# The heads' input projection in pairs of tiles, the last 512 tokens by one level of Strassen's scheme, with four token groups and four shared PSUM banks

## The chip, the cores and the metric

The kernel runs on one core of one Trainium2 chip. The metric is the device time of one execution in microseconds (us), the median over runs. PE is TensorE's matmul side (PEld its weight loads), DVE is VectorE, ACT is ScalarE, POOL is GpSimd, SP is SyncE. A "raw" number is float32. The kernel holds each float32 operand of the projection as two float32r tiles, `hi` (the value rounded) and `lo` (the rest), and a product is three matmuls: hi·hi, hi·lo and lo·hi.

## What is computed

One decoder layer over 1040 tokens (16 meta tokens and 1024) of width 1024. The input projection `proj = a @ w_in` gives 28 tiles of 128 columns: dq, dk, dv (differential attention, four heads each) and hq, hf, hi, hg (HGRN, four heads each). Everything behind it stays as it was.

```python
a = rmsnorm(h, ln_mix_pre[l])
proj = a @ w_in[l]
dq, dk, dv, hq, hf, hi, hg = jnp.split(proj, SPLITS, axis=-1)
y_diff = diff_attention(dq, dk, dv, diff_lambda[l], diff_subln[l], rel_bias_table, lam_init)
y_hgrn = hgrn2(hq, hf, hi, hg, lb_all[l], hgrn_gnorm[l])
mix = jnp.concatenate([y_diff, y_hgrn], axis=-1) @ w_out[l]
h = h + rmsnorm(mix, ln_mix_post[l])
a = rmsnorm(h, ln_ffn_pre[l])
y = conv_ffn(a, w_ffn_up[l], ffn_conv_w[l], ffn_conv_b[l], w_ffn_down[l])
h = h + rmsnorm(y, ln_ffn_post[l])
```

## The kernel before, in words

The tokens stand in nine blocks (16 meta tokens, then eight of 128). For the projection they form three groups of columns, `GROUPS`: blocks 0 to 2 (272 columns), 3 to 5 and 6 to 8 (384 each). The normed input lies transposed in `ahi` and `alo`, eight slabs `k` of 128 rows. A projected tile is a 128-column stripe of `w_in`: for each group 8 slabs × 3 matmuls into one PSUM bank (`proj_group`, line 236, and `proj_step`, line 244), then the tile's own evacuation (`ev_q`, `ev_k`, `ev_v`, `ev_f`, `ev_i`, `ev_g`), which copies the bank to SBUF on ScalarE and VectorE. Values are turned to token rows by transposes afterwards (`to_nat`, line 376; PSUM tile `pn_va` or `pn_vh`), through a list `late` that `flush` empties.

The work has these stages.

The prologue (up to 51.23 us) loads x and the weights, norms the input group by group, and makes dq, dk, dv of head 0 at the same time. Its order is written out by hand and kept on all engines (`state["ordered"]`). For each group: `x_stats` squares the rows on ScalarE and takes the root there (`rstd_of`), the diagonals `dg` are made on ScalarE and VectorE, `x_spread` turns them with a matmul into `prs`, `x_norm` multiplies on VectorE, `x_hi` casts on ScalarE, `x_lo` subtracts on GpSimd. `Kinds` holds the three tiles' matmuls.

The heads (51.23 to 489 us) alternate: four phases of attention with the tiles hf, hq, hi, hg of the same head as dense work, and three phases of HGRN with dq, dk, dv of the next head. `interleave` (line 65) takes a step of the side work, then as many dense matmuls as the fill `FA` = 840 or `FH` = 800 allows, each charged max(115, 0.42 × columns). `dense` (line 791) loads and splits the next tile's weights (`load_split`: cast on ScalarE, subtraction on GpSimd) one tile ahead. PE's order is the order in which the program issues (`manual_schedule`); the other engines get a scheduler's order, and each runs its list in that order. In the heads PSUM holds two banks for the projected tiles (`ip`), two for the small matmuls of the sides (`m`), and two double banks for scores (`S`; block 8's last 512 keys are `E`).

An attention step for block i is: scores S on PE, near-diagonal bias added on VectorE, maximum on VectorE, exponential on ScalarE to `pb`, scaling of pb on VectorE, transposes `pt` on PE, copies `at`, products `pa` on PE. An HGRN step multiplies `kr` and `hq` on VectorE and feeds small matmuls `pl`.

The out-projection, FFN up and FFN down follow; the change does not touch them. SyncE and GpSimd issue the sums of down weights (`tsc`) during the heads.

Of the kernel before, what the change touches and what calls it, by code (L numbers as in the profile page):

```python
# [17 lines left out]
P = 128  # L18
# [12 lines left out]
GROUPS = [(0, 3), (3, 6), (6, 9)]  # L31
# [4 lines left out]
WARM = 26  # L36

# [7 lines left out]


def place(t):
    return t + (0 if t < start(3) else 16)
# [43 lines left out]
def layer_kernel(ctx: ExitStack, tc: tile.TileContext, x, meta, xt, relative, lbl, gpre, gpost, win,  # L92
# [23 lines left out]
    deep = {"ip": 3, "m": 5}  # L116
# [28 lines left out]
    def ps_in(name):  # L145
        return pp.tile([P, 512], F32, tag="ip", name=name, bufs=deep["ip"])

    def ps_m(name):
        return pp.tile([P, 512], F32, tag="m", name=name, bufs=deep["m"])
# [47 lines left out]
    gap(atp, "edge", 64)  # L197
    ahi, alo = (atp.tile([P, KD, P * NBLK], F32R, tag=t, name=t) for t in ("ahi", "alo"))
# [34 lines left out]
    def load_m(m, name, where=None, bufs=4):  # L233
        return [load_split(win[m][:, 512 * c: 512 * (c + 1)], f"{name}_{c}", where, bufs) for c in range(2)]

    def proj_group(g, parts, name, evac):
        b0, b1 = GROUPS[g]
        t0, t1 = start(b0), start(b1 - 1) + P
        n = t1 - t0
        pt = ps_in(f"pi_{name}_{g}")  # L240
        for k in range(KD):
            yield from proj_step(pt[:, :n], parts, k, t0, t1, lambda: evac(g, b0, b1, t0, t1, pt[:, :n]))

    def proj_step(pt, parts, k, t0, t1, evac):
        cost = max(115.0, 0.42 * (t1 - t0))
        hi, lo = parts[k // 4]
        s = slice(P * (k % 4), P * (k % 4 + 1))
        ts = slice(place(t0), place(t0) + t1 - t0)
        T.matmul(pt, hi[:, s], ahi[:, k, ts], start=(k == 0), stop=False)
        yield cost  # L250
        T.matmul(pt, hi[:, s], alo[:, k, ts], start=False, stop=False)
        yield cost
        T.matmul(pt, lo[:, s], ahi[:, k, ts], start=False, stop=(k == KD - 1))
        if k == KD - 1:
            evac()
        yield cost
# [6 lines left out]
    def open_xt(g):  # L263
        b0, b1 = GROUPS[g]
        w = KD * (start(b1 - 1) + P - start(b0))
        raw = mix_tile("X1", F32, "xr0") if g == 0 else zp.tile([P, w], F32, tag=f"xr{g}", name=f"xr{g}", bufs=1)
        xr.append(raw[:, :w].rearrange("p (k t) -> p k t", k=KD))

    def span(g):
        b0, b1 = GROUPS[g]  # L270
        return start(b0), start(b1 - 1) + P
# [4 lines left out]

    def cols(g):
        t0, t1 = span(g)
        return slice(place(t0), place(t0) + t1 - t0)
# [4 lines left out]
    def x_stats(g, on_vector=()):  # L284
        blks = range(*GROUPS[g])
        ss = zp.tile([P, 3], F32, tag="ss", name=f"ss{g}", bufs=3)
# [32 lines left out]
    def x_hi(g, k):  # L319
        return A.copy(ahi[:, k, cols(g)], xr[g][:, k])  # L320

    def x_lo(g, k, eng):
        return eng.tensor_tensor(alo[:, k, cols(g)], xr[g][:, k], ahi[:, k, cols(g)].bitcast(F32), op=ALU.subtract)
# [80 lines left out]

    def hgrn_in(h):
# [4 lines left out]
            "q": long_tile(f"hq{h}")[:, :L],  # L410
# [18 lines left out]
        def ev_g(g, b0, b1, t0, t1, pt):  # L429
            if g == 0:  # L430
                t["gate"] = hp.tile([P, L], F32, tag="gate", name=f"gate{h}")
            s = hp.tile([P, 384], F32, tag="sg", name=f"sg{h}_{g}")[:, : t1 - t0]
# [3 lines left out]
        return t, [(16 + h, f"hf{h}", ev_f), (12 + h, f"hq{h}", ev_q), (20 + h, f"hi{h}", ev_i), (24 + h, f"hg{h}", ev_g)]  # L436
# [5 lines left out]
    def hgrn_head(t, done=None):  # L442
# [5 lines left out]
        a32 = hp.tile([P, 384], F32, tag="sg", name=f"a32{h}")[:, :256].rearrange("p (n c) -> p n c", n=8)  # L448
# [84 lines left out]
        def chain(g):  # L533
            b0, b1 = GROUPS[g]
# [40 lines left out]

        chains = [chain(g) for g in range(3)]
# [54 lines left out]
    def attn_in(h):  # L631
# [27 lines left out]
        return (qs, ks, vn, rr), [(h, f"dq{h}", ev_q), (4 + h, f"dk{h}", ev_k), (8 + h, f"dv{h}", ev_v)]  # L659
# [174 lines left out]
    for i in (3, 4, 5):  # L834
        load_x(i)
# [939 lines left out]
```

## Time and profile before

| | |
|---|---|
| median of 3 runs | 1271.02 us (1270.95 to 1272.37) |
| profiled execution | 1270.04 us, span 1268.2 us |
| granted TensorE clock | 0.999 |
| prologue | 0 to 51.23 us |
| attention phases, with hf, hq, hi, hg | 72.06, 72.51, 72.46, 71.63 us |
| HGRN phases, with dq, dk, dv | 49.70, 49.71, 49.70 us |
| PE, DVE, ACT, POOL busy in the seven phases (437.77 us) | 437.47, 257.27, 252.08, 128.61 us |

A row of a timeline gives start and duration in us, engine, line, operation, the program's names of output and inputs, and the shape. Matmuls overlap, so a duration is longer than the step from one start to the next; the step is what PE pays. A group row gives the count, the busy time and the mean in ns of one, then the idle time ahead of it and what ended it. Most rows of DVE, ACT and POOL stand on line 59, the helper that issues for these engines, so they are told apart by the names.

### The profile page before, as it was taken

The page shows a single profiled execution, that of the slowest core. Times are in us where ns is not written, and L with a number is a line of the kernel's source. Part 1 is how long each engine was busy: PE and PEld are TensorE (multiplying, and loading weights), DVE is VectorE, ACT ScalarE, POOL GpSimd, SP SyncE. Part 2 cuts the span into 40 slices and gives each one's busy share as a digit, 9 for nine tenths or more (in the row PEclk, how much of TensorE's full clock was granted, in tenths as well). Part 3 has the DMA queues.
Part 4 walks back from the last instruction along what each step waited for, and adds up shares of the span by engine and source line. Part 5 has one row for each costly group of instructions (what it writes and reads, how often), then busy time and mean ns, then how long its engine had stood idle before and what let it go on. Part 6 is the DMA issues. An engine that isn't in the chain of part 4 may idle for free.

```text
span 1268.2 us, 26069 instructions
## 1 busy us (share of the span) xinstructions
PE 1254.6 (99%) x10168; PEld 1174.9 (93%) x10168; DVE 912.7 (72%) x1504; ACT 685.4 (54%) x1632; POOL 512.0 (40%) x396
## 2 busy tenths in 40 slices
PE   9999999999999999999999999999999999999997
PEld 8999999999999998778999999999999998878886
DVE  6764646565655564558899888889898877797586
ACT  7765466547644763456764544544445544564554
POOL 5442323333213311353067677677676731020111
PEclk9999999999999999999999999999999999999999
DMA  8554564464633534787222222222222247955363
GB/s 322 170 104 100 98 140 83 98 125 118 115 99 68 125 94 128 237 278 273 85 76 72 80 92 68 92 92 68 92 77 75 76 136 259 343 184 167 92 216 125
DMA packets 117599, 169.30 MB, mean 133 GB/s; under 512 B 10258, under 2 KB 57938, under 8 KB 117476
## 3 DMA queue, kind: packets, MB, share of 16 engines
q1 hardware_dynamic: 94244, 156.10, 37.7%
q0 software_dynamic: 23232, 11.54, 7.7%
q8 instruction: 80, 1.31, 0.4%
q14 instruction: 43, 0.35, 0.1%
HBM read 138.50 MB, written 52.17 MB: 150 GB/s over the span
## 4 chain that ended last, share of the span: by engine, by line
PE 83%; DMA 6%; DVE 4%; ACT 3%; issue 1%; POOL 1%; SPq 1%; DVEq 0%; ACTq 0%; POOLq 0%
PE pb L1426 5%; PE pb L1425 5%; PE pb L1427 4%; PE pd L1600 4%; PE pd L1601 4%; PE pd L1599 4%; PE pa L759 3%; PE pa L1426 3%; PE pc L1426 3%; PE pa L1425 3%; PE pc L1425 3%; PE pc L1427 3%; PE pa L1427 3%; DMA ra<-in_wup_dram 2%; PE pt L735 2%; DMA gi<-gsc 1%
## 5 line engine op out<-in xcount | busy, mean ns | idle before, releaser
L1425 PE MATMUL pb<-t,uh 128*128 128x258 f32 x504 | 140.6, 279 | 0.8 <-DVE u L59 0.8
L1426 PE MATMUL pb<-t,uh 128*128 128x258 f32 x504 | 140.9, 280 | 0.3 <-DVE t L59 0.3
L1427 PE MATMUL pb<-t,ul 128*128 128x258 f32 x504 | 140.1, 278 | 0.0
L1600 PE MATMUL pd<-wl,gh 128*128 128x512 f32 (+1 forms) x312 | 121.0, 388 | 1.2 <-DVE wl L59 1.2
L1599 PE MATMUL pd<-wh,gh 128*128 128x512 f32 (+1 forms) x312 | 120.8, 387 | 0.5 <-DVE x L59 0.5
L1601 PE MATMUL pd<-wh,gl 128*128 128x512 f32 (+1 forms) x312 | 120.7, 387 | 0.0
L59 DVE SCALAR_TENSOR_TENSOR c<-uu,cwt,c 128x514 f32<-128x514 f32 (+1 forms) x88 | 106.9, 1215 | 0.0
L59 DVE SCALAR_TENSOR_TENSOR c<-ug,cwt,c 128x514 f32<-128x514 f32 (+1 forms) x88 | 101.5, 1154 | 0.0
L59 ACT ACTIVATE c<-c 128x514 f32<-128x514 f32 (+1 forms) x44 | 27.9, 634 | 130.1 <-DVE c L59 130.1
L1425 PEld LDWEIGHTS pb<-t,uh 128*128 128x128 f32 x504 | 94.8, 188 | 1.0 <-DVE u L59 1.0
L1426 PEld LDWEIGHTS pb<-t,uh 128*128 128x128 f32 x504 | 94.8, 188 | 0.6 <-DVE t L59 0.6
L1427 PEld LDWEIGHTS pb<-t,ul 128*128 128x128 f32 x504 | 94.8, 188 | 0.0
L1426 PE MATMUL pa<-t,uh 128*128 128x258 f32 (+1 forms) x336 | 93.9, 279 | 0.0
L1426 PE MATMUL pc<-t,uh 128*128 128x258 f32 (+1 forms) x336 | 93.9, 279 | 0.0
L1425 PE MATMUL pa<-t,uh 128*128 128x258 f32 (+1 forms) x336 | 93.6, 279 | 0.0
L1425 PE MATMUL pc<-t,uh 128*128 128x258 f32 (+1 forms) x336 | 93.6, 278 | 0.0
L1427 PE MATMUL pa<-t,ul 128*128 128x258 f32 (+1 forms) x336 | 93.4, 278 | 0.0
L1427 PE MATMUL pc<-t,ul 128*128 128x258 f32 (+1 forms) x336 | 93.4, 278 | 0.0
L59 POOL TENSOR_TENSOR ul<-ws,uh 128x512 fp32r<-128x512 f32 x42 | 69.2, 1647 | 59.6 <-PE pa L1427 43.9
L59 POOL TENSOR_TENSOR ws<-ra,ra 128x512 f32<-128x512 f32 x42 | 67.8, 1615 | 61.0 <-DMA ra<-in_wup_dram 33.9
L59 POOL TENSOR_TENSOR c<-c,c 128x514 f32<-128x514 f32 (+1 forms) x44 | 68.5, 1558 | 54.2 <-ACT c L59 49.5
L59 DVE TENSOR_TENSOR ul<-ra,uh 128x512 fp32r<-128x512 f32 x43 | 41.6, 967 | 46.6 <-POOL ul L59 46.6
(386 smaller groups left out, 4179.8 us busy)
## 6 DMA issues: line engine op xcount, KB each, us to landing
ra<-in_wup_dram SPq DMA_DIRECT2D x88, 256.0 KB, 2.6
mp<-msc SPq DMA_DIRECT2D x23, 512.0 KB, 5.6
tsc<-in_wdown_dram SPq DMA_DIRECT2D x44, 256.0 KB, 5.6
wi<-tsc SPq DMA_DIRECT2D x44, 256.0 KB, 3.0
gi<-gsc SPq DMA_DIRECT2D x33, 256.0 KB, 4.0
wi<-in_wdown_dram SPq DMA_DIRECT2D x33, 256.0 KB, 5.3
gsc<-c SPq DMA_DIRECT2D x22, 257.0 KB, 2.0
tsc<-in_wdown_dram POOLq DMA_DIRECT2D x22, 256.0 KB, 6.7
```

The costliest lines, as they stand in the source:

```text
L59: ins = call(*args, **kw)
L735: T.transpose(pt[:b, jj * r:(jj + 1) * r], pb[:r, 0, start(j):start(j) + b], ident[:r, :r])
L759: T.matmul(po[:, :P], w_, vn[:, j], start=(j == 0), stop=(j == i))
L1425: T.matmul(pt, hi[:, s], th[:, k], start=(first and k == 0), stop=False, skip_group_check=True)
L1426: T.matmul(pt, hi[:, s], tl[:, k], start=False, stop=False, skip_group_check=True)
L1427: T.matmul(pt, lo[:, s], th[:, k], start=False, stop=(k == 3), skip_group_check=True)
L1599: T.matmul(py, gh[:, s], wh, start=(k == 0 and pr not in (3, 7)), stop=False, skip_group_check=True)
L1600: T.matmul(py, gh[:, s], wl, start=False, stop=False, skip_group_check=True)
L1601: T.matmul(py, gl[:, s], wh, start=False, stop=(k == NH - 1), skip_group_check=True)
```

## The change

There are four groups: 272 columns and three of 256. The first two are kept as `g0` and `g1`, the last two as four quarters by slabs and columns: b11 (slabs 0 to 3, group 2), b21 (slabs 4 to 7, group 2), b12 and b22 (the same for group 3).

Tiles come in pairs (hf with hq, hi with hg, dk with dq). With A and B the two weight stripes, halved by slabs into a1, a2, b1, b2, the last 512 columns of both tiles are a 2 × 2 block product, and it takes seven products of 12 matmuls instead of eight. The products use sums of raw weights (`G.tensor_tensor` four times a pair, on GpSimd), cast on ScalarE and with lows on VectorE (`prepare`), and sums of raw inputs t1 to t4, made once at the prologue's end. Their results are put together from PSUM by five sums on VectorE. The first 528 columns go plainly. dv alone has no partner and goes plainly (`one_tile`). The operand t3 takes the place of b12 after the prologue.

In the heads all projected tiles and small matmuls share one tag of four PSUM banks. The HGRN query gets a tile of its own, because its old place holds t4. The HGRN chains keep their three groups (`CHAINS`). `flush` comes ten matmuls after something is put on `late`. In the prologue the fourth group has its own statistics, spread, norm and splits.

```diff
-GROUPS = [(0, 3), (3, 6), (6, 9)]
+GROUPS = [(0, 3), (3, 5), (5, 7), (7, 9)]
+CHAINS = [(0, 3), (3, 6), (6, 9)]
+HW = 256
+FLUSH = 10
-    deep = {"ip": 3, "m": 5}
+    banks_of = {"ip": ("ip", 3), "m": ("m", 5)}
...
-    deep.update(ip=2, m=2)
+    banks_of.update(ip=("x", 4), m=("x", 4))
...
+    left = halves_tile("g0", [KD, META + 2 * P]), halves_tile("g1", [KD, HW])
+    op = {nm: halves_tile(nm, [KD // 2, HW]) for nm in ("b11", "b21", "b22", "b12")}
...
+    def two(ms, names, evacs):
+        (mA, mB), (nA, nB), (eA, eB) = ms, names, evacs
+        a1, a2 = (part_of.pop((mA, c)) for c in range(2))
+        b1, b2 = (part_of.pop((mB, c)) for c in range(2))
+        r11, r12, r21, r22 = (raw_of.pop((m, c)) for m in ms for c in range(2))
+        G.tensor_tensor(r22, r21, r22, op=ALU.add)
+        G.tensor_tensor(r21, r11, r21, op=ALU.subtract)
+        G.tensor_tensor(r11, r22, r11, op=ALU.subtract)
+        G.tensor_tensor(r12, r12, r11, op=ALU.subtract)
+        sums = {}
+
+        def prepare(j, raw):
+            sums[j] = slot(f"s{j}_{mA}")
+            split(*sums[j], raw, V)
+            load_next()
+
+        x1, u2, w5 = (tmp[:, HW * n: HW * (n + 1)] for n in range(3))
+        yield from left_chunk(0, (a1, a2), nA, eA)
+        pa = bank(f"{nA}_a")
+        yield from product(pa, a1, op["b11"], True, True)
+        A.copy(x1, pa)
+        yield from left_chunk(1, (a1, a2), nA, eA, lambda: prepare(2, r11))
+        yield from product(pa, a2, op["b21"], False, True)
+        eA(2, 5, 7, *span(2), pa)
+        prepare(1, r22)
+        yield from left_chunk(0, (b1, b2), nB, eB)
+        pb = bank(f"{nB}_b")
+        yield from product(pb, sums[2], op["t2"], True, True)
+        V.tensor_tensor(u2, pb, x1, op=ALU.add)
+        prepare(3, r21)
+        pc = bank(f"{nB}_c")
+        yield from product(pc, sums[1], op["t1"], True, True)
+        V.tensor_tensor(w5, pc, u2, op=ALU.add)
+        prepare(4, r12)
+        yield from left_chunk(1, (b1, b2), nB, eB, split_next)
+        pd = bank(f"{nB}_d")
+        yield from product(pd, sums[3], op["t3"], True, True)
+        V.tensor_tensor(w5, pd, w5, op=ALU.add)
+        split_next()
+        yield from product(pc, sums[4], op["b22"], False, True)
+        V.tensor_tensor(x1, pc, u2, op=ALU.add)
+        eA(3, 7, 9, *span(3), x1)
+        split_next()
+        yield from product(pd, b2, op["t4"], False, True)
+        V.tensor_tensor(u2, pd, u2, op=ALU.add)
+        eB(2, 5, 9, span(2)[0], L, tmp[:, HW:])
+        split_next()
...
+    stats = x_stats(3)
+    for kd in second:
         kd.out()
-    dq, dk, dv = [Kinds(j, 2, ps_in) for j in range(3)]
+    dq, dk = third = [Kinds(j, 2, ps_in) for j in range(2)]
...
+    spread[3] = x_spread(3, stats)
+    for k in range(KD):
+        last_norm = x_norm(3, k, spread[3])
+        last_hi = x_hi(3, k)
+        x_lo(3, k, G)
+    flush()
...
+    f2, f3 = xr[2], xr[3]
+    G.tensor_tensor(f2[:, :4], f3[:, :4], f2[:, :4], op=ALU.subtract)
+    V.tensor_tensor(f3[:, :4], f3[:, 4:], f3[:, :4], op=ALU.subtract)
+    V.tensor_tensor(f3[:, 4:], f3[:, 4:], f2[:, :4], op=ALU.subtract)
+    for _ in range(4):
+        split_next()
+    G.tensor_tensor(f2[:, 4:], f2[:, 4:], f3[:, 4:], op=ALU.subtract)
...
+    for nm, src in (("t2", f3[:, 4:]), ("t1", f2[:, :4]), ("t3", f3[:, :4]), ("t4", f2[:, 4:])):
+        split(*op[nm], src, V)
```

The first place where the order changes is PE's list in the prologue. Before, around the spread of the third group (prs; dg are the diagonals, pi_dq_1 the second group of dq, alo its low parts), the rows are:

```order
88 L862 MATMUL pi_dv_1_373<-ahi,w_126 128x384 x2
89 L312 MATMUL prs_459<-dg_441,ones 128x128
90 L312 MATMUL prs_459<-dg_443,ones 128x128
91 L312 MATMUL prs_459<-dg_445,ones 128x128
92 L862 MATMUL pi_dq_1_371<-alo,wh_dq_0_156 128x384 x4
93 L862 MATMUL pi_dq_1_371<-alo,wh_dq_1_160 128x384 x4
94 L382 MATMUL pn_va_0_495<-ident,vt_0_457 128x128
95 L384 MATMUL pn_va_0_495<-ident,vt_0_457 128x128 x2
96 L862 MATMUL pi_dk_1_372<-alo,wh_dk_0_158 128x384 x4
```

That was the last spread. After, PE's list has one more, ahead of the third group's low products (b11l, b21l) and followed by the transposes of the second group's values:

```order
128 L975 MATMUL pi_dk_2_545<-b21h,wh_dk_1_172 128x256
129 L975 MATMUL pi_dk_2_545<-b21h,wl_dk_1_173 128x256
130 L414 MATMUL prs_578<-dg_528,ones 128x128
131 L414 MATMUL prs_578<-dg_530,ones 128x128
132 L486 MATMUL pn_va_1_605<-ident,vt_1_542 128x128 x2
133 L975 MATMUL pi_dq_2_544<-b11l,wh_dq_0_166 128x256 x4
134 L975 MATMUL pi_dq_2_544<-b21l,wh_dq_1_170 128x256 x4
135 L975 MATMUL pi_dk_2_545<-b11l,wh_dk_0_168 128x256 x4
```

What moved: a second spread and a pair of transposes now stand between the third group's high and low products.

The second place is ScalarE's list where the heads begin. Before (wh are weight casts, vt the last values, kr the first step of hf's evacuation, pb_0 the first block's exponentials):

```order
47 L59 CAST k_0_120<-pi_dk_2_530 64x384
48 L59 CAST k_0_121<-pi_dk_2_530 64x384
49 L59 CAST k_0_120<-k_0_120 64x384
50 L59 CAST k_0_121<-k_0_121 64x384
51 L59 CAST wh_hq_1_707<-wr_hq_1_706 128x512
52 L59 COPY vt_2_640<-pi_dv_2_531 128x384
53 L59 COPY avn_122<-pn_va_2_747 128x384
54 L59 ACTIVATE pb_0_732,ast_0_733<-S_0_734,ast_0_733 16x16 x2
55 L59 ACTIVATE kr_684<-pi_hf_0_716 128x272
```

After (t_790, t_791 and t_792 are the operands t2, t1 and t4; xr_451 and xr_277 the raw sums):

```order
56 L58 CAST wh_1_727<-wr_1_652 128x512
57 L58 COPY vt_2_757<-pi_dv_2_732 128x256
58 L58 ACTIVATE le<-le 128x2
59 L58 COPY avn_132<-pn_va_2_776 128x256
60 L58 COPY vt_3_788<-pi_dv_3_759 128x256
61 L58 CAST t_790<-xr_451 128x1024
62 L58 CAST t_791<-xr_277 128x1024
63 L58 CAST b12h<-xr_451 128x1024
64 L58 CAST t_792<-xr_277 128x1024
65 L58 COPY avn_132<-pn_va_3_871 128x256
66 L58 ACTIVATE kr_846<-pi_hf_0_860 128x272
67 L58 COPY tmp<-pi_hf_a 128x256
```

What moved: four casts of 1024 columns stand between the last values and the first evacuation of hf, and the first block's exponentials come after both. VectorE's list has the four lows at the same place, ahead of the first block's bias.

The third place is VectorE's list in the first attention phase, at blocks 3 and 4 (S_3 and S_4 are scores with their bias, ast their maxima, pb the probabilities). Before:

```order
80 L59 COPY at_1_0_852<-pt_1_0_851 128x128
81 L59 TENSOR_TENSOR S_3_864<-S_3_864,rr_124 128x2x256
82 L59 TENSOR_TENSOR ona_0_836<-ona_0_836,nssa_0_837 16x128
83 L59 TENSOR_REDUCE ast_3_863<-S_3_864 128x2
84 L59 SCALAR_TENSOR_TENSOR nssa_3_1045<-ast_3_863 128x1
85 L59 RECIPROCAL ast_3_863<-ast_3_863 128x1
86 L59 SCALAR_TENSOR_TENSOR ast_3_863<-ast_3_863,nlam 128x1
87 L59 SCALAR_TENSOR_TENSOR pb_3_862<-pb_3_862,ast_3_863 128x400
88 L59 TENSOR_SCALAR kr_684<-kr_684 128x384
89 L59 TENSOR_TENSOR S_4_0_934<-S_4_0_934,rr_124 128x256
```

After, wl_s are the lows of summed weights and tmp the sums from PSUM:

```order
92 L58 TENSOR_REDUCE ast_3_1039<-S_3_1040 128x2
93 L58 TENSOR_TENSOR wl_s_16_1029<-wr_1_652,wh_s_16_1028 128x512
94 L58 SCALAR_TENSOR_TENSOR nssa_3_1233<-ast_3_1039 128x1
95 L58 TENSOR_TENSOR S_4_0_1095<-S_4_0_1095,rr_134 128x256
96 L58 RECIPROCAL ast_3_1039<-ast_3_1039 128x1
97 L58 TENSOR_REDUCE ast_4_1094<-S_4_0_1095 128x1
98 L58 SCALAR_TENSOR_TENSOR ast_3_1039<-ast_3_1039,nlam 128x1
99 L58 COPY at_2_0_1079<-pt_2_0_1078 128x256
100 L58 SCALAR_TENSOR_TENSOR pb_3_1038<-pb_3_1038,ast_3_1039 128x400
101 L58 TENSOR_TENSOR tmp<-pi_hq_b,tmp 128x256
102 L58 TENSOR_TENSOR wl_s_16_1119<-wr_0_650,wh_s_16_1118 128x512
```

What moved: lows of weights and sums from PSUM stand between the steps of the score chains.

More of the change, by code (lines that the diff above doesn't have):

```diff
@@ L244, in proj_step @@
[L244 to L256, printed above, removed]
+        return start(b0), start(b1 - 1) + P
@@ L931, in layer_kernel @@
     for half in range(2):
[L932 removed]
+        dv.part(half, 0, 1)
     x_norm(1, 0, spread[1])
```

271 lines of the change are left out of this document (181 added, 90 removed).

## The prediction

> **What bounds the kernel now.** I read the busy times first, then a table of engine times by stage, then the PE timeline of single stretches for the spacing of the matmuls. The profiled run took 1270.04 us, 1.8 over its span; the runs' median is 1271.02, so a time on the profile's scale becomes one on the runs' scale by adding 1.0.
>
> The page, and the table by stage (windows cut where a head's first dense tile starts; columns: length, then busy us of PE, PEld, DVE, ACT, POOL, granted clock, DMA share, GB/s):
>
> ```profile
> span 1268.2 us, 26069 instructions
> PE 1254.6 (99%) x10168; PEld 1174.9 (93%) x10168; DVE 912.7 (72%) x1504; ACT 685.4 (54%) x1632; POOL 512.0 (40%) x396
> 51.23:123.29 72.06, 72.06 (x502) 70.80 (x502) 41.20 (x98) 43.81 (x134) 20.46 (x17) 1.00 0.46 108
> 172.99:245.50 72.51, 72.51 (x505) 71.16 (x505) 42.91 (x101) 45.62 (x138) 21.83 (x19) 1.00 0.51 109
> 245.50:295.21 49.71, 49.61 (x732) 47.15 (x732) 28.97 (x59) 23.98 (x67) 18.16 (x20) 1.00 0.56 106
> ```
>
> PE is busy 72.51 of 72.51 us in an attention phase (hf, hq, hi, hg under attention) and 49.61 of 49.71 in a phase of HGRN (the next head's dq, dk, dv under it): the heads run as fast as PE issues. Every microsecond of matmul taken out counts, as long as the others keep up: in an attention phase VectorE stands at 42.91 / 72.51 = 59% and ScalarE at 63%.
>
> **What PE saves.** The spacing of matmuls by width, from starts on the PE timeline (start, duration, engine, line, operands); the 256-column rows are from the FFN:
>
> ```profile
> 173.12 0.28 PE L251 MATMUL pi_hf<-alo,wh_hf 128*128 128x272 f32 x1
> ...
> 174.59 0.29 PE L251 MATMUL pi_hf<-alo,wh_hf 128*128 128x272 f32 x1
> 183.02 0.33 PE L249 MATMUL pi_hf<-ahi,wh_hf 128*128 128x384 f32 x1
> ...
> 183.88 0.34 PE L253 MATMUL pi_hf<-ahi,wl_hf 128*128 128x384 f32 x1
> 184.19 0.42 PE L249 MATMUL pi_hf<-ahi,wh_hf 128*128 128x384 f32 x1
> 901.50 0.28 PE L1425 MATMUL pb<-t,uh 128*128 128x256 f32 x1
> ...
> 902.74 0.28 PE L1427 MATMUL pb<-t,ul 128*128 128x256 f32 x1
> 115.20 2.01 PE pa L759 x18
> ```
>
> 272 columns: (174.59 − 173.12) / 12 = 0.1225, by longer stretches 0.123; 384: 0.86 / 5 = 0.172, by longer ones 0.173; 256: 1.24 / 11 = 0.113. A pair of tiles is 48 matmuls of 272 and 96 of 384 before: 5.90 + 16.61 = 22.51 us. After, it is 48 of 272, 48 of 256 for the second groups and 7 products of 12, 84 of 256: 5.90 + 132 × 0.113 = 20.82. So −1.69 a pair, and there are 4 + 4 + 3 = 11: −18.6. A tile alone (dv, three times) goes from 48 of 384 to 72 of 256: 8.30 − 8.14 = −0.16, −0.5 in all; the three tiles before the heads the same, −0.5. Against this, a switch from a side step back to a dense tile lengthens the first matmul (184.19: 0.42 beside 0.34), and I count 182 such places in the new order against 172: +0.8. PE alone: −18.6 − 0.5 − 0.5 + 0.8 = −18.8.
>
> By the isolated gap that the Trainium skill gives ("TensorE: Matmul & The Clock Gate", Back-to-back issue gap: N / 2.4 + 2.5 ns) 256, 272 and 384 columns would be spaced 109, 116 and 162.5 ns, a pair would save an estimated 1.2 us and the 11 pairs 13 instead of 18.6. The rows here are 113, 123 and 172 ns, so I go by them.
>
> **What the prologue loses.** Here ScalarE's queue decides. Its rows of before, VectorE's diagonals, and PE's rows at the same place (start, duration):
>
> ```profile
> 22.67 4.19 ACT L59 CAST ahi<-xr 128x384 fp32r<-128x384 f32 x8 [1.82 <-DVE xr L59]
> 26.76 1.05 ACT L59 ACTIVATE x<-x 128x1024 f32<-128x1024 f32 x1
> 30.02 0.30 ACT L59 ACTIVATE ss<-ss,eps 128x3 f32<-128x3 f32 x1
> 30.35 0.20 ACT L59 ACTIVATE ss<-ss 128x3 f32<-128x3 f32 x1
> 30.89 0.78 ACT L59 ACTIVATE q<-pi_dq 64x272 fp32r<-64x272 f32 x2
> 31.70 0.78 ACT L59 CAST k<-pi_dk 64x272 fp32r<-64x272 f32 x2
> 32.38 0.86 ACT L59 CAST k<-k 64x272 fp32r<-64x272 f32 x2
> 33.27 0.39 ACT L59 COPY vt<-pi_dv 128x272 f32<-128x272 f32 x1
> 38.28 0.52 ACT L59 COPY avn<-pn_va 16x128 f32<-16x128 f32 x2
> 31.32 0.35 DVE L59 TENSOR_SCALAR dg<-ident,ss 128x128 f32<-128x128 f32 x2
> 23.23 0.45 PE L862 MATMUL pi_dq<-ahi,wh_dq 128*128 128x384 f32 x1 [0.25 <-ACT ahi L59]
> 32.28 0.83 PE L312 MATMUL prs<-dg,ones 128*128 128x128 f32 x6
> 34.35 0.27 PE L382 MATMUL pn_va<-ident,vt 128*128 128x128 f32 x1
> ```
>
> Before, vt of the first group was ready at 33.66 and PE asked for it at 34.35: 0.7 to spare. Now the second group has 48 high products of 0.113 instead of 0.173, and PE comes 48 × 0.06 + 8 × 0.06 = 3.4 sooner, 0.2 more with a block fewer in prs (30.8), while ScalarE saves only a Square (1.05) and 8 × 0.12 on narrower casts (4.19 / 8 = 0.52 at 384, 0.39 for the copy of 272, so about 0.40 at 256), and delivers at 31.7: a wait of 0.9. The third group's casts (8 × 0.40), two Squares (2.1), the rstd (0.6) and the two diagonals on VectorE (0.35) then stand ahead of prs3, which the new order puts ahead of that group's low products on PE: 31.7 + 3.2 + 0.5 (avn) + 2.1 + 0.6 + 0.35 = 38.4, and PE, at 31.7 + 18 × 0.113 + 32 × 0.113 = 37.4, waits 1.0. Next on PE is pn_va of the second group; its vt stands on ScalarE behind six q and k evacuations: 38.1 + 2.4 + 0.4 = 40.9 against 38.9 on PE, 2.0. The last pn_va0_2 waits behind four casts of weights, about 0.6. Together 4.5, and nothing on PE's queue passes a waiting matmul. Bounds: 2 (the casts beat their estimates and the last two vanish) and 7 (the extra x loads for four groups come late).
>
> **What the start of the heads loses.** Four raw differences are split into 128x1024 operands (t2, t1, b12, t4). Their casts stand on ScalarE, and their lows on VectorE, ahead of S0_0 and its exponential. The nearest rows for 1024 columns and the rows of the first block's chain:
>
> ```profile
> L59 ACT ACTIVATE pb<-S,ast 128x912 f32<-128x912 f32 x8 | 8.2, 1022 | 5.2 <-DVE ast L59 5.2
> L59 DVE TENSOR_TENSOR hq<-hq,f 128x1040 f32<-128x1040 f32 x3 | 3.7, 1231 | 0.0
> 45.83 1.29 POOL L59 TENSOR_TENSOR wl_hf<-wr_hf,wh_hf 128x512 fp32r<-128x512 f32 x1 [3.16 <-PE pi_dq L862]
> L59 POOL DMA_DIRECT2D tsc<-in_wdown_dram x22 | 29.8, 1664 | 0.0
> 53.50 0.19 DVE L59 TENSOR_TENSOR S<-S,rr 16x32 f32<-16x32 f32 x1 [2.95 <-PE S L679]
> 55.50 0.22 DVE L59 SCALAR_TENSOR_TENSOR pb<-pb,ast 16x16 f32<-16x16 f32 x1
> 58.13 0.18 PE L735 MATMUL pt<-ident,pb 16*16 16x16 f32 x1
> ```
>
> The heads start near 51.2 + 4.5 − 0.5 = 55.2. PE reaches pt0_0, the transpose of the first block, 58.13 − 51.23 = 6.9 later, 62.1. The cast of t4 waits for a GpSimd sum of 128x1024 (2.5, about twice a 128x512), which stands on POOL behind four lows of weights (1.3 each) and a DMA issue (1.66). The first of these lows follows its cast, which stands on ScalarE behind the q and k evacuations, now 512 columns wide, that follow dq's and dk's low products near 48.5; I put it at 52: 52 + 4 × 1.3 + 1.7 + 2.5 = 61.4. Cast 1.1, low 1.2: 63.7. Then S0_0's sum, maximum, two exponentials and pb's scaling, 2.2 as before (the sum starts at 53.50, pb's scaling ends at 55.72): 65.9. PE waits 3.8, with all later work of the stage behind pt0_0. Bounds: 1 (POOL early) and 6.
>
> **What the heads lose.** Per pair the other engines get four raw sums (POOL), four casts (ACT), four lows and five sums from PSUM (VectorE), a copy and one more evacuation. Prices:
>
> ```profile
> L59 DVE TENSOR_TENSOR ul<-ra,uh 128x512 fp32r<-128x512 f32 x43 | 41.6, 967 | 46.6 <-POOL ul L59 46.6
> L59 DVE TENSOR_TENSOR S<-S,rr 128x256 f32<-128x256 f32 x32 | 13.7, 427 | 6.4 <-PE S L679 6.4
> L59 ACT CAST wh_hg<-wr_hg 128x512 fp32r<-128x512 f32 x8 | 5.0, 622 | 2.4 <-issue 1.7 <-PE pi_hq L251 0.8
> 219.55 1.02 ACT L59 ACTIVATE pb<-S,ast 128x912 f32<-128x912 f32 x1 [0.58 <-DVE ast L59]
> 220.71 0.49 PE L678 MATMUL E<-k,q 128*128 128x512 f32 x1
> 258.08 0.69 DVE L59 TENSOR_TENSOR hq<-hq,tt 128x520 f32<-128x520 f32 x1
> 259.35 0.70 PE L489 MATMUL pl<-hq,kr 128*32 128x16 f32 x62
> ```
>
> An attention phase (two pairs) adds 8 × 0.97 + 10 × 0.43 = 12.0 to VectorE, 8 × 0.62 + 2 of evacuations = 7 to ScalarE; its length falls by 3.4 to 69.1. VectorE rises to 54.9 / 69.1 = 79%, ScalarE to 76%: not full, but each queue runs in order. PE's tightest spot per head is block 8's E, which reuses a bank that an exponential leaves at 219.55 + 1.02 = 220.57, 0.14 before PE writes it at 220.71. A low of weights standing ahead of that chain costs 0.97 − 0.14 = 0.83: over four heads 3.3. In an HGRN phase the tight spot is hq ready at 258.77 against pl at 259.35, 0.58 to spare; one low there costs 0.4, over three phases 1.2. Sum 4.5. Bounds: 0, if the lows fall between chains; and 13.5, if a low and a PSUM sum (1.4) stand at two spots of each phase, 4 × 2 × 1.25 + 3 × 2 × 0.6. The four shared banks add a bound of the same kind: a tile then waits for whichever of four the queue frees last, and I take it as within the 13.5.
>
> **The sum.** 1270.0 − 18.8 + 4.5 + 3.8 + 4.5 = 1264.0, on the runs' scale 1265. The rest of the layer is the same code; 0.
>
> **The rivals.**
> *Cover holds.* The helpers' lows fall into VectorE's free 41% and PE waits only where the prologue's bounds force it (2 + 1): 1270.0 − 18.8 + 3 = 1254, on the runs' scale 1255; for it speaks that PE did not wait in the heads with ScalarE at 63%. Chance 0.22.
> *The in-order queues bind in the heads.* At 79% VectorE, lows and PSUM sums stand before S, E and pl chains at most blocks. It decides from 18.8 − 4.5 − 3.8 = 10.5 us of waits in the heads, 1.5 a phase; at its bound of 13.5 and the prologue's upper bounds (7 + 6), 1270 − 18.8 + 13.5 + 13 = 1278; typically 1275 on the runs' scale. Against: E and pl are among the tightest spots of their phases, and PE waited at neither. Chance 0.22. By the Trainium skill ("SBUF — State Buffer", SBUF: two separate sides) a VectorE operation with two SBUF inputs and a GpSimd operation shut each other out for whole instructions; an estimate by it would give each low another 1.3 us. The row of ul, 0.97 with GpSimd's own lows going on beside it, does not show a whole GpSimd operation added.
> *A matmul costs a fixed part, so more and narrower ones lose.* The 128-column row of the chain, 2.01 / 18 = 0.112, costs as much as 256 columns. If the 256-column matmuls here cost what 272 do, 0.123, the gain shrinks by 0.010 × (11 × 132 + 6 × 72) = 18.8, to nothing: 1270 + 4.5 + 3.8 + 4.5 = 1283. The FFN's 256-column rows speak against it. Chance 0.04. The Trainium skill's sustained figures (same section: about 81 ns at 128 columns and 131 at 512) are such a rule, and an estimate by the line through them is 17.7 us a pair against 15.8 before; no row here agrees with them.
>
> **How the numbers follow.** The forecast, waits at three places and a net gain, has chance 0.52, with its own range 1259 to 1271. A change under 0.2% (2.5 us, about what a measurement of this kernel can tell) is 1268.5 to 1273.5. Faster by more: the first rival 0.22 and 0.39 of the forecast, 0.61. Within: 0.13 of the forecast and 0.03 of the queues rival, 0.16. Slower: 0.19 + 0.04 = 0.23. The range, 1254 to 1277, takes in most of the first two rivals and leaves out the third.
>
> **What would show it.** On PE's timeline of the new kernel: spacing 0.113 at 256 columns in the heads (else the third rival); gaps before pn_va0_0, prs3, pn_va0_1, and one of some 3 to 4 us before pt0_0; the head phases at 69 and 48 us plus waits, with PE's idle time ahead of E and pl and VectorE as its releaser; VectorE near 79% there. I am wrong if PE waits nowhere in the prologue, or if the idle time in the heads passes 10 us.

## The result: 1331 us, 4.7% slower, and the profile after

| | before | after |
|---|---|---|
| median of 4 runs each | 1271.26 us (1270.95 to 1272.37) | 1331.16 us (1330.52 to 1332.04) |
| ratio of the two, with its 95% interval | | 1.047 [1.0452, 1.0488] |
| profiled execution, span | 1268.2 us | 1328.7 us |
| granted TensorE clock over the span | 0.999 | 0.984 |

The forecast was 1265, in a range of 1254 to 1277. The change went the other way, and the time lies outside the range. First the page of the new kernel:

```profile
span 1328.7 us, 27548 instructions
PE 1261.9 (95%) x10708; PEld 1181.7 (89%) x10708; DVE 1013.3 (76%) x1630; ACT 726.4 (55%) x1752; POOL 582.2 (44%) x450
```

PE stood still for 13.6 us of the span before (1268.2 − 1254.6); now for 66.8. The table by stage (prologue, the seven phases in turn, all behind the heads; columns as in the prediction: length, busy us of PE, PEld, DVE, ACT, POOL, granted clock, DMA share, GB/s):

```profile
0.00:56.29 56.29, 51.02 (x377) 48.45 (x378) 39.95 (x93) 40.30 (x95) 30.89 (x48) 0.97 0.69 240
56.29:144.00 87.71, 73.15 (x574) 71.72 (x573) 68.03 (x124) 52.79 (x155) 37.50 (x29) 0.92 0.34 76
144.00:198.96 54.96, 50.32 (x794) 48.53 (x793) 37.80 (x71) 28.14 (x81) 22.08 (x22) 0.97 0.48 108
198.96:277.64 78.68, 72.55 (x578) 70.86 (x576) 54.92 (x120) 51.27 (x155) 32.03 (x27) 0.98 0.47 99
277.64:332.12 54.48, 50.13 (x795) 48.37 (x793) 41.29 (x71) 28.04 (x81) 24.62 (x24) 0.97 0.52 101
332.12:410.56 78.44, 72.56 (x577) 70.88 (x576) 54.58 (x120) 51.38 (x155) 32.04 (x27) 0.98 0.48 98
410.56:464.98 54.42, 50.18 (x795) 48.50 (x794) 40.74 (x71) 28.03 (x81) 21.95 (x22) 0.97 0.43 92
464.98:546.00 81.02, 74.51 (x577) 72.54 (x576) 57.25 (x121) 50.55 (x153) 27.01 (x22) 0.96 0.36 84
546.00:1328.70 782.70, 767.44 (x5660) 701.81 (x5658) 618.78 (x840) 395.90 (x805) 354.11 (x233) 1.00 0.43 141
```

An attention phase went from 72.5 to 78.7 us, an HGRN phase from 49.7 to 54.5, the first attention phase from 72.06 to 87.71. By parts, the span grew by 60.5: the prologue +5.1, the first attention phase +15.7, the other six phases +35.2 (the out-projection starts at 546.0; before, at 490.05), and all behind +4.6. PE's idle time in the seven phases is their 489.71 less the busy 443.40, so 46.3; before it was 0.3. Taken over a whole phase, neither VectorE nor ScalarE is full, and the granted clock is below 1 in every phase.

What PE waited for in the heads (us in total, times, longest):

```profile
PE pa L868 <- ACT az L58: 11.4, 6, 2.8
PE pt L844 <- DVE pb L58: 11.3, 1, 11.3
PE pl L597 <- DVE hq L58: 7.5, 4, 2.5
PE E L787 <- ACT pb L58: 7.2, 4, 2.1
PE pi_dk L278 <- DVE am L58: 3.9, 3, 1.7
```

One wait of 11.3 at the start of the heads, then a few of 1 to 3 us in each phase, at E and pl as the prediction named them, and at pa and pi_dk, which it did not.

**The start of the heads.** GpSimd's, VectorE's and ScalarE's rows of that place, the first transpose on PE, and the clock beside it (in the last fence the windows of 2 us end in clock, DMA share and GB/s):

```profile
61.05 2.91 POOL L58 TENSOR_TENSOR xr<-xr,xr 128x1024 f32<-128x1024 f32 x1
...
64.23 8.85 POOL L58 TENSOR_TENSOR wr<-wr,wr 128x512 f32<-128x512 f32 x4
```

```profile
59.01 8.54 DVE L58 TENSOR_TENSOR t<-xr,t 128x1024 fp32r<-128x1024 f32 x2
67.47 2.28 DVE L58 TENSOR_TENSOR b12l<-xr,b12h 128x1024 fp32r<-128x1024 f32 x1
69.68 2.28 DVE L58 TENSOR_TENSOR t<-xr,t 128x1024 fp32r<-128x1024 f32 x1
71.98 0.19 DVE L58 TENSOR_TENSOR S<-S,rr 16x32 f32<-16x32 f32 x1
```

```profile
63.99 1.04 ACT L58 CAST t<-xr 128x1024 fp32r<-128x1024 f32 x1 [3.27 <-POOL xr L58]
```

```profile
74.31 0.18 PE L844 MATMUL pt<-ident,pb 16*16 16x16 f32 x1 [11.34 <-DVE pb L58]
```

```profile
68.00:70.00 2.00, 0.00 (x0) 0.00 (x0) 2.00 (x2) 0.00 (x0) 1.92 (x2) 0.50 0.14 17
78.00:80.00 2.00, 2.00 (x12) 2.00 (x11) 0.80 (x3) 0.78 (x4) 0.00 (x0) 0.50 0.34 122
```

The cast of t4 ends at 65.0, and the prediction put its low 1.2 behind that. VectorE was still at the second low. The last two take 2.28 each while GpSimd adds raw weights beside them (64.23 to 73.08); the first two took 8.54 together, beside GpSimd's lows of weights, its sum of raw inputs and its first sum of raw weights. ScalarE's cast takes 1.04 at the same place, as in the forecast (1.1). So the first block's bias starts at 71.98 instead of 63.7. The clock then halves: PE is idle from 63.0 to 74.3, the clock is at 0.50 in the window from 68, and still there up to 80, almost 6 us after PE is busy again.

**An attention phase.** ScalarE's rows, VectorE's low of the summed weight, and PE's rows at the same place:

```profile
210.64 0.62 ACT L58 CAST wh_s<-wr 128x512 fp32r<-128x512 f32 x1 [2.08 <-POOL wr L58]
211.16 0.16 ACT L58 COPY az<-pt 16x16 f32<-16x16 f32 x1
...
213.34 0.51 ACT L58 ACTIVATE kr<-kr,one 128x256 f32<-128x256 f32 x1 [1.75 <-DVE kr L58]
```

```profile
211.29 1.22 DVE L58 TENSOR_TENSOR wl_s<-wr,wh_s 128x512 fp32r<-128x512 f32 x1 [0.52 <-ACT wh_s L58]
```

```profile
211.37 0.49 PE L868 MATMUL pa<-avn,az 128*128 128x128 f32 x2 [1.39 <-ACT az L58]
218.25 0.49 PE L868 MATMUL pa<-avn,az 128*128 128x128 f32 x2 [2.45 <-ACT az L58]
```

The cast of a summed weight stands at the head of ScalarE's list and waits 2.08 for GpSimd's sum; the copy az, 0.16 long, whose input PE wrote at 207.24, stands behind it, and PE's pa waits 1.39 for az. The second wait of pa, 2.45, is not ScalarE waiting for GpSimd: the late cast makes VectorE's low late, which takes 1.22 beside GpSimd's sums, VectorE's kr stands behind that low, ScalarE waits 1.75 for kr, and from 213.34 it works without a pause up to the next az at 217.96. Over the heads, GpSimd's sums ended 22.7 us of ScalarE's idle time ahead of the casts:

```profile
L58 ACT CAST wh_s<-wr 128x512 fp32r<-128x512 f32 x44 | 27.2, 619 | 45.7 <-POOL wr L58 22.7 <-PE pi_dk_a L278 6.6 <-PE pi_dq_b L278 4.8
```

### The profile page after: what moved, and what is told of

The parts are those of the page before. It is cut to its first block, busy times and chain, and to the rows that moved or that the text cites. A ratio compares the mean times of both kernels' runs of the same rounds, so it can differ in the third digit from the quotient of the medians.

```text
span 1328.7 us, 27548 instructions
## 1 busy us (share of the span) xinstructions
PE 1261.9 (95%) x10708; PEld 1181.7 (89%) x10708; DVE 1013.3 (76%) x1630; ACT 726.4 (55%) x1752; POOL 582.2 (44%) x450
## 4 chain that ended last, share of the span: by engine, by line
PE 45%; DVE 3%; ACT 2%; DMA 1%; issue 1%; SPq 0%; DVEq 0%; ACTq 0%
PE pd L1762 5%; PE pd L1763 5%; PE pd L1761 4%; PE pb L1588 4%; PE pb L1587 4%; PE pb L1589 4%; PE pa L1588 3%; PE pc L1588 3%; PE pa L1587 3%; PE pc L1587 3%; PE pc L1589 3%; PE pa L1589 3%; DVE xh L58 1%; DMA gi<-gsc 1%; ACT a L58 1%
## 5 line engine op out<-in xcount | busy, mean ns | idle before, releaser
L58 POOL TENSOR_TENSOR wl<-wr,wh 128x512 fp32r<-128x512 f32 x50 | 68.9, 1387 | 188.9 <-ACT wh L58 151.1
```

What stands on the lines that cost most here:

```text
L58: ins = call(*args, **kw)
```

## The experiments

The theories, by the letters that some of the expectations use. P: GpSimd's raw sums cost the time, by arriving late for ScalarE's in-order list and by shutting out VectorE. L: VectorE and ScalarE have too much work in all. B: the four shared banks make tiles wait for one another. C: a wait of PE lets the clock fall, and the slow clock costs time of its own. The other parts to tell apart are the narrower groups and the scheme itself. Ratios are to the kernel before, run on the same chip, with 95% intervals.

**e1_sums_on_vector.** The four raw sums of a pair go to VectorE.

```diff
-        G.tensor_tensor(r22, r21, r22, op=ALU.add)
...
+        V.tensor_tensor(r22, r21, r22, op=ALU.add)
...
```

> The four raw weight sums of a pair go from GpSimd to VectorE; PE's order is the same. Theory P (GpSimd's sums make the waits: ScalarE's casts of the sums wait for them at the head of its queue, and VectorE's operations with two SBUF inputs are shut out while GpSimd runs them): the 45 us of PE waits in the heads fall to about 15 and the 11.3 us at the start of the heads to about 6, so 1290 to 1305 us against 1331. Theory L (VectorE and ScalarE have too much work in all): VectorE gets 11 x 4 x 0.7 = 31 us more, so 1331 to 1350. Theory B (four shared banks and narrower chunks): 1331, the banks are the same.

1304.77 us, 1.0264 [1.0238, 1.029]: 26 us less than with GpSimd, as P has it and against L, although VectorE has 44 operations more. The clock over the span is 0.991. The first wait is 9.7 where about 6 was expected.

**e2_sums_unused and e3_no_sums.** In both, ScalarE and VectorE split raw weights instead of their sums, so that the layer's result is another. In e2 GpSimd still makes sums of nearly the same size (496 of 512 columns), into a tile that nobody reads; in e3 there are none.

```diff
-        G.tensor_tensor(r22, r21, r22, op=ALU.add)
...
+        spill = hp.tile([P, 496], F32, tag="spill", name=f"spill_{mA}")
+        for u, v in ((r21, r22), (r11, r21), (r22, r11), (r12, r11)):
+            G.tensor_tensor(spill, u[:, :496], v[:, :496], op=ALU.add)
```

> GpSimd still does four sums of a pair (496 columns), but writes them to a tile that nobody reads; the casts take the raw weights instead of the sums, so the result is not the layer's. ScalarE then never waits for a sum, while VectorE is shut out as before. If the wait at the head of ScalarE's queue carries theory P: about 1300. If shutting VectorE out carries it: 1318 or more. Theories L and B: 1331, the work is the same.

> The four raw weight sums are left out altogether, the casts take the raw weights, so the result is not the layer's; casts, lows, PSUM sums and banks stay. Theory P: 1280 to 1292, the floor that the rest of the change allows. Theory L: 1320 or more, as neither VectorE nor ScalarE loses work. Theory B: 1325 or more.

e2: 1308.23 us, 1.0289 [1.027, 1.0308]. e3: 1290.95 us, 1.0154 [1.0135, 1.0174]. Three steps follow. From the new kernel to e2, −22.9: nobody waits for a sum any more. PE's waits in the heads fall from 11.4 to 2.6 at pa for az, from 8.8 to 1.3 at pl for hq, from 7.2 to 3.7 at E, and from 3.9 to 0.5 at pi_dk. From e2 to e3, −17.3: GpSimd's 44 sums cost that much though nobody reads them; of the 20.8 between the two profiled executions 14.4 lie in the heads and 6.0 behind them. From e3 to before, −19.7: what is left without any sums of weights. In the profiled execution that is 4.5 in the prologue, 7.9 in the first attention phase, 2.0 in the first HGRN phase, 0.7 in the other five phases and 3.5 behind the heads. There the four lows at the start (VectorE's timeline of e3) still meet GpSimd's one sum of inputs, then take the 1.21 that the prediction had assumed; and a later attention phase is as long as before:

```profile
58.50 6.03 DVE L58 TENSOR_TENSOR t<-xr,t 128x1024 fp32r<-128x1024 f32 x2
64.46 1.21 DVE L58 TENSOR_TENSOR b12l<-xr,b12h 128x1024 fp32r<-128x1024 f32 x1
```

```profile
187.36:259.87 72.51, 70.78 (x577) 69.30 (x576) 50.24 (x120) 51.15 (x155) 21.45 (x19) 1.00 0.50 107
```

PE is busy 1.7 us less than the 72.51 of before and idle 1.7: PE's gain is there, half of the 3.4 forecast for two pairs, and is used up in the same phase.

**e10_before_idle_sums.** The other way round: the kernel before, with the sums added to GpSimd, unread.

```diff
+            if idx + 1 < len(tiles) and idx % 2 == 0:
+                spill = hp.tile([P, 512], F32, tag="spill", name=f"spill_{name}")
+                for u in range(4):
+                    with tc.issue_after(lows[-1].ins):
+                        G.tensor_tensor(spill, ahi[:, u, 288:800].bitcast(F32), alo[:, u, 288:800].bitcast(F32), op=ALU.add)
```

> The kernel before, with four GpSimd operations of 128x512 per two projected tiles added (44 in all, two SBUF inputs, output to a tile that nobody reads), behind the weight lows on GpSimd's queue; nobody waits for them but GpSimd's own next work. If GpSimd's work shuts VectorE out (theory P, second half): VectorE's operations with two SBUF inputs beside them take 1.2 to 2.5 us instead of 0.55 to 1.2, PE waits in the heads, and the time rises by 5 to 17 us, as e2 against e3 (17). If VectorE is not shut out, or has cover enough: 1271 to 1273.

1287.81 us, 1.0134 [1.0115, 1.0153]: +16.6, close to e2 − e3. Its groups on VectorE in the heads, then the same operations before:

```profile
L59 DVE TENSOR_TENSOR kr<-kr,f 128x520 f32<-128x520 f32 x3 | 5.4, 1786 | 0.0
L59 DVE SCALAR_TENSOR_TENSOR pb<-pb,ast 128x784 f32<-128x784 f32 x4 | 7.1, 1776 | 0.1
L59 DVE TENSOR_TENSOR S<-S,rr 128x256 f32<-128x256 f32 x32 | 13.6, 425 | 2.5 <-PE S L679 2.4
```

```profile
L59 DVE TENSOR_TENSOR kr<-kr,f 128x520 f32<-128x520 f32 x3 | 2.1, 695 | 0.0
L59 DVE SCALAR_TENSOR_TENSOR pb<-pb,ast 128x784 f32<-128x784 f32 x4 | 4.1, 1034 | 0.1
```

The operations with two inputs in SBUF grow from 0.70 to 1.79 and from 1.03 to 1.78. The bias S<-S,rr, with one of its inputs in PSUM, stays at 0.43. Half of what PE then waits for (e10, heads; 13.2 us in all):

```profile
PE E L678 <- ACT pb L59: 4.9, 4, 1.9
PE pl L489 <- DVE hq L59: 1.9, 1, 1.9
```

These are the two spots that the prediction had found tight in before, now reached without a single operation of the change on VectorE or ScalarE.

**e5_before_four_banks.** The kernel before with the heads' small tiles in one tag of four banks, for B.

```diff
-        return pp.tile([P, 512], F32, tag="ip", name=name, bufs=deep["ip"])
+        return pp.tile([P, 512], F32, tag=shared[0] if shared else "ip", name=name, bufs=deep["ip"])
...
-    deep.update(ip=2, m=2)
+    deep.update(ip=4, m=4)
+    shared.append("x")
```

> The kernel before, with nothing changed but the PSUM tags of the heads: the projected tiles and the small matmuls share four banks instead of two and two. The waits for a bank in the changed kernel (pi_dk behind VectorE's am, 3.9 us) stand on late VectorE work by theory P: 1269 to 1273. If the shared banks make waits by themselves (theory B): 1276 or more.

1269.0 us over ten runs, 0.9986 [0.9973, 1.0]. Shared banks cost the kernel before nothing, and of the new kernel's 3.9 us of waits at pi_dk e2, with the same banks, keeps 0.5: B falls. They bring nothing that this measurement could tell from zero either.

**e4_plain_four_groups.** The new kernel without the scheme: four groups, shared banks, tiles one at a time, every product plain.

```diff
-        return [((16 + h, 12 + h),), ((20 + h, 24 + h),)]
+        return [((m + h,),) for m in (16, 12, 20, 24)]
...
-        yield from left_chunk(1, ws, name, evac)
-        yield from product(pa, w2, op["b21"], False, True)
...
+        for g in range(4):
+            yield from left_chunk(g, ws, name, evac)
```

> No Strassen: every tile alone and plainly in four groups (24 x (0.123 + 3 x 0.113) us on PE), no sums of weights or inputs, no operands t1 to t4; the prologue's four groups, the four shared banks, the feed of weights and FLUSH stay. Theories P and L: 1270 + 4.5 to 5 of prologue - 3 = 1272 to 1278. Theory B: 1295 or more, most of the loss stays.

1285.55 us, 1.0112 [1.0094, 1.0129], more than the 1272 to 1278 expected. The heads start at 58.0, and the attention phases take 72.4 to 72.8, but the HGRN phases 51.9 to 53.7 instead of 49.7. PE's longest group of waits in the heads, and the row of the second HGRN phase in the table by stage:

```profile
PE pl L586 <- issue: 3.9, 2, 2.1
```

```profile
254.71:308.33 53.62, 51.42 (x807) 49.93 (x805) 30.63 (x64) 24.77 (x76) 17.67 (x20) 0.97 0.54 105
```

PE pauses among the small matmuls of pl with nothing that the profile shows to wait for; one such pause, from 265.07, lasts 1.78 us. The phase has 807 matmul records where before had 732; four groups instead of three make 72 of the difference. What the pauses are stays open. The two longer of the three phases also have a clock of 0.97, an estimate of 1.6 us each; the third, at 51.9, has 1.00.

**e9_busy_in_first_wait and e11_busy_shorter.** For C: matmuls of the identity that fill PE's first long wait, 90 in e9, 26 in e11. Their bank is overwritten by the transposes that follow.

```diff
+                if h == 0 and i == 0:
+                    for _ in range(26):
+                        T.matmul(pt[:, :P], ident, ident, start=True, stop=True)
```

> The changed kernel, with 90 more matmuls of 128x128 in front of the first block's transposes (some 10 us, within the wait of 11.3 us there; they are overwritten). If the granted clock of 0.50 from 68 to 80 us follows from PE's idle time and costs time after it (theory C: a wait costs its length and then about 6 us at half speed), the clock stays at 1.00 and the time falls by about 3 us, 1331 to 1328, the first phase from 87.7 to about 84.7. If the clock is no cause, 1331 to 1332 and the first phase stays at 87.7.

> As e9, with 26 matmuls instead of 90: in e9 each of them ran as two of 0.11 us and the 90 took 22 us, twice the wait. 26 take about 6 us, at half clock for the first 3.5, so some 8 us from the moment that their bank is free (9.9 us after the heads start), and end about when the first block's pb is ready. Theory C: the clock is back at 1.00 before the first transposes, the first phase falls from 87.7 to about 85, the time by 2 to 3 us. If the half clock after the wait costs nothing: 87.7 and 1331.

e9: 1340.9 us, 1.0543 [1.0523, 1.0564]. Each of its matmuls ran as two, together 22 us, twice the wait, so the time of e9 tells little about C. e11: 1327.72 us (1322.1 to 1329.29), 1.0438 [1.0416, 1.0461], with 52 matmuls in 7.70 us, inside the wait:

```profile
67.18 7.70 PE L844 MATMUL pt<-ident 128*128 128x128 f32 x52 [3.23 <-ACT avn L58]
```

```profile
78.00:80.00 2.00, 2.00 (x18) 2.00 (x17) 1.30 (x8) 1.95 (x10) 0.00 (x0) 1.00 0.46 131
```

The clock is back at 1.00 from 72 on, where the new kernel has 0.50 up to 80, and the first attention phase takes 84.97 instead of 87.71. Work that computes nothing saves 2.7 us in that phase: C holds, at about 3 us for a long wait. The execution that was profiled is the fastest of e11's four (1322.1); later phases account for the rest of its lead, and the section on the prediction comes back to them.

**e6_sums_on_vector_lead and e8_lead_more_fill.** The remedies: e6 is e1 with more dense matmuls ahead of the first side step; e8 is e6 with a larger fill in the attention phases. The edit of e8 against the new kernel, without e1's part:

```diff
-FA, FH, FO = 840, 800, 740
+FA, FH, FO = 980, 800, 740
...
-        interleave(dense(tiles_h, wd_sums), [attn(h, t_a)] + carried(), FA, 1500)
+        interleave(dense(tiles_h, wd_sums), [attn(h, t_a)] + carried(), FA if h else 800, 1500 if h else 9500)
```

> As e1 (raw weight sums on VectorE), and in the first attention phase PE takes dense matmuls worth 9500 units first instead of 1500, some 70 matmuls or 8 us, before it comes to the first block's transposes. If the 9.7 us wait at the start is only lateness of the four splits of 1024 columns, that wait falls below 2 us and the time from 1305 to about 1296; the dense work is then missing at the end of the phase, where 6 us of it were left over, and should cost 0 to 3. If the splits hold something else up (banks that ScalarE must empty), the wait only moves: 1303 or more.

> As e6, and the fill of the attention phases rises from 840 to 980 (800 in the first), so that the dense matmuls left over at a phase's end (6 to 8 us) stand between the steps instead. If the waits left in the attention phases (az 1 to 2 us, E 1 us) are a lack of cover, they vanish: 4 to 8 us less than e6, about 1289. If they stand on the order of the queues: as e6.

e6: 1303.96 us, 1.0254 [1.0239, 1.0269], as e1. The wait for the first pb is gone, and PE waits in the same stage instead for the cast of a sum, for tmp (1.7) and for VectorE's ona (2.5), so the wait only moved (e6, heads):

```profile
PE pi_hq_c L278 <- ACT wh_s L58: 4.0, 1, 4.0
```

e8: 1298.45 us, 1.0214 [1.019, 1.0237], 5.5 less than e6, within the 4 to 8 expected. It is the fastest with the whole scheme, and still 28 us slower than before. Its later attention phases take 71.6 to 72.2 and its HGRN phases 50.0 to 50.1, as long as before, so the gain on PE is used up there too. The loss lies in the prologue (4.9), behind the heads (6.4) and above all in the first attention phase, 16.2 longer than before:

```profile
56.11:144.40 88.29, 77.41 (x575) 74.48 (x574) 65.73 (x131) 52.23 (x153) 25.85 (x22) 0.92 0.34 75
```

**e7_ticks_after_sums.** GpSimd's DMA issues (tsc) are moved behind the sums, within a pair, to take them out of the sums' way.

```diff
-            for _ in ms:
-                next(side, None)
...
+                if n == (120 if len(ms) == 2 else 1):
+                    for _ in ms:
+                        next(side, None)
```

> The changed kernel with GpSimd's sums, but the issue of the down weights' DMA sums (two of GpSimd's four per pair) moves behind the raw weight sums of the pair. If GpSimd is late with the sums because of these DMA issues, ScalarE's waits for a sum (2.1 us in an attention phase, 4.8 in an HGRN phase) shrink by about 2 each and the time falls from 1331 to 1312 to 1320. If the sums' own time (four of 1.3 to 2 us) makes them late: 1326 to 1333.

1342.58 us, 1.0578 [1.054, 1.0615]. The edit did not do what it was for: in GpSimd's trace the issues came between the sums, one and one, from 199.7 to 209.4. The first sum of that pair started 1.4 us sooner, counted from the lows ahead of it, and the waits moved to other spots. What the DMA issues cost the sums stays open.

## Why the prediction was wrong, point by point

**The spacing was right, PE's saving too large.** A stretch of 256-column matmuls in the heads of the new kernel:

```profile
273.28 0.28 PE L278 MATMUL pi_hg_d<-b12h,wh_s 128*128 128x256 f32 x1
...
275.89 0.28 PE L278 MATMUL pi_hg_c<-b22h,wl_s 128*128 128x256 f32 x1
```

2.61 us over 23 steps is 0.1135, as forecast, and not the 0.123 of 272 columns: the third rival, a fixed cost of each matmul, falls. But the heads are not made of such stretches. Take the mean step from one dense matmul to the next record of the same tile, over the last six phases: before 0.1313 at 272 columns and 0.1850 at 384; in e3, where the clock is full there, 0.1333 at 272 and 0.1239 at 256. With these a pair saves 48 × 0.1313 + 96 × 0.1850 − 48 × 0.1333 − 132 × 0.1239 = 1.31 us instead of 1.69, and 11 pairs 14.4 instead of 18.6. Every width costs 0.008 to 0.012 more among the side steps than in an unbroken row, and the scheme has 36 more dense matmuls in a pair. The +0.8 for ten more switches was mis-sized: these steps put it near 4.

**The prologue was right in its waits, and by luck near in its length.** Its waits now, against 0.9, 1.0, 2.0 and 0.6 forecast:

```profile
PE pn_va L486 <- ACT vt L58: 2.1, 2, 1.5
PE prs L414 <- DVE dg L58: 0.8, 1, 0.8
PE pn_va L484 <- ACT vt L58: 0.7, 1, 0.7
```

They add up to 3.6 against 4.5. The heads start 5.06 later, where 4.0 was the sum of the terms: the clock fell in the prologue too (0.97 over it, an estimate of 1.7 us), which no term held.

**The start of the heads: right place and chain, 11.3 instead of 3.8.** The step that failed is the price of the lows, 1.2 each with GpSimd taken as idle behind its own part of the chain. GpSimd went straight on to the first pair's sums. In e3, without these, the later lows take 1.21 and the wait is 6.6, still over the bound of 6; there the second of the first two lows, beside GpSimd's sum of raw inputs, is the long one.

**What the heads lose: 4.5 forecast, at most 13.5; PE's idle time there was 35.0 beside the first wait (46.3 − 11.3).** This is the step that decided, and the prediction's own sign of being wrong, more than 10 us of idle time in the heads, came true. The added work on VectorE and ScalarE was priced; GpSimd's sums were counted only as four operations on an engine that nobody waits for. The experiments give them two prices: 17 us for being there (e2 − e3, and e10), through the operations of VectorE that they stretch; and 23 us for being late (the new kernel − e2), through ScalarE's in-order list. Part of both is the clock: from the new kernel to e2 the heads get 25.9 shorter in the profiled executions, with 18.0 less of PE's idle time and 7.9 less of its busy time.

VectorE's total of 54.9 us a phase was met (54.92 in the second attention phase) by accident: the 44 lows of the sums were cheaper than the 0.97 assumed, at a median of 0.69 and at most 1.24, and older operations took what they left, as in e10. As a share it was 70% and not 79%, since the phase did not get shorter.

The prediction had set the shutting-out aside with this sentence: "The row of ul, 0.97 with GpSimd's own lows going on beside it, does not show a whole GpSimd operation added." The row was a mean. The spread of the same group of before does show it (minimum, median and maximum in ns):

```profile
L59 DVE TENSOR_TENSOR ul<-ra,uh x43: 677/682/1772, 551.5 to 1025.1; 128x512 fp32r<-128x512 f32 x43
```

At least half of these 43 cost 0.68, and some cost up to 1.1 us more, nearly one GpSimd low of weights (1.29). The Trainium skill ("SBUF — State Buffer", SBUF: two separate sides) says that a VectorE operation with two SBUF inputs and a GpSimd operation that reads SBUF share a pair of ports by an exclusive lock, held for the whole instruction. The traces here agree: 0.70 becomes 1.79 with two inputs in SBUF (kr), and 0.43 stays with one in PSUM (S).

**The clock was not in the prediction at all.** By the table by stage, the time that the clock held back in the seven phases is the sum of (1 − clock) × length: 7.0 + 4.9 + 3.1 + 3.2 = 18.2, by clocks rounded to 0.01, so give or take 2.5. Some of that fell while PE was idle, 3.8 of it at the start, so busy PE lost at most some 14. The trace shows single falls: the long one at the start and seven of 3.4 us each, each behind a wait of 1.7 to 2.8 us. e11 prices one of them. Its phases three to six do the same work with nearly the same waits, and there the clock did not fall; this is the first of them:

```profile
196.11:273.33 77.22, 71.15 (x577) 69.48 (x576) 54.60 (x120) 51.15 (x155) 32.15 (x28) 1.00 0.48 99
```

The new kernel has 78.68, with PE busy 72.55. Over the four phases PE is busy 1.4 to 1.6 us longer where the clock fell. Seven falls and the 2.7 at the start make an estimate of 12.5 to 14 us. This is most of why PE's busy time in the heads did not fall but rose, from 438.5 (437.47 and the last 1.05 up to 490.05) to 443.4: the 14.4 saved against some 13 lost would leave it 1 lower. Another estimate comes from how busy time is counted. The last matmul before a wait counts at its whole length (0.28 at 62.69), not at its step of 0.11; at 27 waits that is 4.6 us. Some 1 to 2 us stay without a cause that a run showed. The Trainium skill ("TensorE: Matmul & The Clock Gate", What's actually happening) puts the fall to half clock after an idle window of about 3.4 us and the return after about 3.4 us of sustained work. The fall at the start agrees (idle from 63.0, 0.65 in the window from 66 to 68, then 0.50). The return took almost 6 us in the new kernel, and the seven later falls came behind shorter waits; there the measurement decides.

**Behind the heads, 0 forecast, +4.6 measured.** PE's waits as the out-projection begins (woh 1.7, wol 1.1 and 0.5, on 1.2) add up to 4.5 us, against 1.1 before. The sums of weights are not the main part: e3, without them, still has +3.5 there, and e4, without the scheme, +0.1. Which part of the scheme brings them was not tried.

**The rivals.** "The in-order queues bind in the heads" was nearest: the queues did bind, at E, pl and behind the casts. But its price had a ceiling of 13.5 because it counted only the lists that got new work. "Cover holds" fell in the heads: VectorE had free time, and PE waited all the same.

What stays open: the pauses inside pl in e4, which have no releaser in the profile (with its clock they cost an HGRN phase 2 to 4 us); what the DMA issues cost the sums; and whether e8 would come near the kernel before if its first attention phase lost its 16 us, which no run tried. No version here is faster than the kernel before by more than these runs can tell, e5 included, and e8, the best with the scheme, is 2.1% slower.

## What to carry to other kernels

An operation on GpSimd that nobody waits for is not free: ask which VectorE operations with two SBUF inputs will run beside it, and price them by the spread of the rows, not by their mean. A cast whose input comes from a slow engine should stand behind, not ahead of, the short copies that PE waits for on the same in-order list; the waits at az say so, and no run here tried that order. When PE has no slack, saving 1.5% of its time in matmuls needs the other engines to keep up at every block, and a wait of some microseconds can be paid a second time in clock. Price many narrow matmuls by their steps among the other work, not by an unbroken row.

## What the runs showed of the hardware

- A single low of 128x1024 lasted 6.4 us (61.15 to 67.55) where e3's later ones take 1.21: it ended only after two GpSimd operations in turn, the sum of raw inputs from 61.05 and the first sum of raw weights from 64.23, not after one.
- The clock also fell behind waits far shorter than the first, but not behind each. PE waits 1.39 and 2.45 within 8 us (up to 211 and 218, above), and the window behind them has the row below. In e11 four waits of 2.4 to 2.5 us in phases three to six were followed by no fall, and in e3's last six phases, with no wait over 1.3, there was none.

```profile
220.00:222.00 2.00, 2.00 (x13) 2.00 (x12) 1.38 (x4) 1.36 (x7) 0.00 (x0) 0.55 0.32 123
```

- At half clock, 256-column matmuls follow one another at 0.213 (rows from 76.77 to 77.41 on PE's timeline), against 0.1135.
- A float32 matmul of 128x128 shows as two records in e11: 26 were issued and 52 recorded, 7.70 / 52 = 0.15 us each, part of them at half clock.
